# Half of the sums over x moved into attention, and gate steps from block 2 on

## The chip, the cores and the metric

The kernel runs on one core of a Trainium2 chip. The metric is the device time of one execution in microseconds; several executions of the kernel before are timed, and their median stands for it. One more execution is recorded by the profiler, and all rows quoted below come from it.

The engines are called as the profile calls them: PE (TensorE, matmuls), PEld (its weight loads), DVE (VectorE), ACT (ScalarE), POOL (GpSimd) and SP (SyncE, which here only issues DMAs). Every engine works through its own list of instructions in order; an instruction that must wait holds up all that stand behind it in that list. POOL both computes and issues DMAs, so a DMA on POOL that waits holds up POOL's arithmetic too.

## The reference, cut to what matters

All arrays are float32; x is 512 positions by 1024 features, one batch, one layer.

```python
h = rms_norm(x, norm_mix_g)
cb, cc, cin, q, k, v, f_logit, g_logit = split(h @ w_in)
u = causal_dwconv(cc * cin, conv_mix_w)              # 3 taps
y_conv = (cb * u) @ w_out_conv                       # 512 -> 1024
o = softmax(q.k / sqrt(64) + F[t] - F[s]) @ v        # s <= t, 8 heads of 64, F = cumsum(log_sigmoid(f))
y_attn = o @ w_out_attn                              # 512 -> 1024
g_conv, g_attn = split(sigmoid(g_logit + b_gate))    # 2 x 1024
x = x + (g_conv * y_conv + g_attn * y_attn) @ w_o
a, b = split(causal_dwconv(rms_norm(x) @ w_up, conv_ffn_w))   # 2 x 2816
x = x + (silu(a) * b) @ w_down
return rms_norm(x)
```

What matters here are the two gate projections: 1024 features in, two times 1024 out. They are computed in eight blocks j of 128 output features; a block needs one 128-wide piece of `g_conv` and one of `g_attn`.

## The kernel before

Features lie on the 128 partitions, positions along the free axis, so x is held as eight slabs of 128 x 512. Every matmul is made precise by splitting both sides into a high and a low part and adding three products (high weight by high x, low weight by high x, high weight by low x; `mm3`, L278, and `passes`, L296). One matmul is a 128x128 weight tile on 256 columns. Of x, scaled by the norm's gains, the high part `xgh` and the low part `xgl` are made once at the start. Weights are streamed by SP in an order fixed by the list `stream`; each chunk lands in one of five buffers `raw`, ACT copies it to `wh` (L245) and DVE subtracts to get `wl` (L249). `wh` and `wl` have two buffers each, so a chunk can be split while the one before it is multiplied. `proj` multiplies one chunk of 128 output features: 48 matmuls.

The stages in order:

1. **Start.** SP asks for `vec` (a table of per-feature constants, with the first half of the first slab of x in it), v weights and x slabs (L409 to L417): first in turn, and from slab 4 on all the rest of x ahead of the rest of the v weights. The v projection runs over the eight slabs.
2. **Attention.** q and k of heads 0 to 3, then 32 units of scores, softmax, transposes and products with v (`scores`, `transp`, `attend`). Between the units `fill` puts the halves of other projections: the conv branch (its products z and y on POOL, L569 and L579; its taps `u` on ACT and DVE, L548), the remaining q and k, and last the two gates of block 0. Three banks of PSUM (0, 1, 2) go round for these projections; before that, q1's result is in bank 0 and k1's in bank 1, and DVE reads q1's with L525 (`t_q`).
3. **Eight mix blocks.** Block j has its two gates, then `yc` (conv branch out) and `ya` (attention out) from the chunk `mix{j}`, then sigmoid, products and their sum (`ml`, `mh`).
4. **Output projection, FFN up, FFN down, final norm**, which this change doesn't touch.

The gates come in two ways. The plain way, blocks 1 and 2 (`GS = 3` is the first block not done so; block 0's gates belong to attention), is two `proj`: 96 matmuls. The other way, blocks 3 to 7 (`gate_pair`), is a 2-by-2 block product with seven products in place of eight (Winograd's form): 84 matmuls. It needs sums over weight blocks and sums over x blocks.

The weight sums are made in DRAM, with no engine: for a group of two steps, SP issues a copy (L132), POOL an accumulating DMA (L135), SP a copy, POOL an accumulating DMA, SP a copy, POOL an accumulating DMA, each one waiting for the one before. One of these six operations is issued at each `tick()`; there is a tick in each of the 32 attention units and then one at some of the weight chunks. The operations of two groups alternate (`zip` over two groups). A gate step then loads its chunk `P` (weights as they are, 384 KB) and its chunk `F` (sums, 512 KB).

The x sums: for each pair q of x slabs (four pairs) `x_load` (L777) asks POOL for the two slabs again from DRAM, `x_forms` scales them on ACT (L782), makes four sums t1 to t4 on DVE (L786 to L789) in a tile `tq`, and splits them into `txh` (ACT, L790) and `txl` (DVE, L791). All of it lies after attention: `x_load(0)` and `x_load(1)` at block 0, `x_forms` of pairs 0 to 3 behind the four plain projections of blocks 1 and 2, one each. The slabs' buffers are of the tag `mt` and can only be used when attention's own tiles have been given back.

The order on each engine is set when the program is built: most instructions keep the order in which the code names them, `after_split()` ties what is named inside it to stand behind the newest weight split, and the rest is ordered by the scheduler.

## Time and profile before

| | |
|---|---|
| runs of the kernel before | 704.12, 705.13, 705.40 us; median 705.13 |
| the profiled execution | 707.72 us, of which the span of the records is 706.0 |
| PE busy | 694.1 us, 98% |
| DVE busy | 494.1 us, 70% |
| ACT busy | 340.2 us, 48% |
| POOL busy | 155.8 us, 22% |
| PE by the chain that ended last | 92% of the span |
| attention with its projections, by the order of PE's rows | to 189.78 us |
| block 1: two plain gates | 189.78 to 204.77 us, 15.0 |
| block 2: two plain gates | 210.21 to 221.09 us, 10.9 |
| block 3: first gate step | 226.53 to 236.05 us, 9.5 |

Times inside the span are counted from its start. Granted clock (PEclk) is the TensorE clock that the throttle granted, 1.00 being full speed. A row of the timeline gives start, duration, engine, line, operation, output and inputs, and in brackets how long the engine was idle before and what ended that; a row of the chain gives start, duration, engine, line and output.

### The profile page before, as it was taken

How to read it: one execution, taken by the hardware profiler on the slowest of the kernel's cores; microseconds unless marked ns; L12 is line 12 of the kernel's file. 1: busy time of each engine (PE TensorE's matmuls, PEld its weight loads, DVE VectorE, ACT ScalarE, POOL GpSimd, SP SyncE). 2: the span in 40 equal slices, each digit the busy share in tenths (PEclk: the TensorE clock that was granted, in tenths of full speed). 3: DMA queues.
4: the chain of work that ended last, by engine and by line, in shares of the span. 5: the costliest groups of instructions: out<-in, count | busy, mean ns of one | idle time of the engine just before them, and what ended most of it. 6: DMA issues, size and time to landing. Idle time of an engine off the chain costs nothing.

```text
span 706.0 us, 14566 instructions
## 1 busy us (share of the span) xinstructions
PE 694.1 (98%) x6017; PEld 692.2 (98%) x6017; DVE 494.1 (70%) x790; ACT 340.2 (48%) x538; POOL 155.8 (22%) x177
## 2 busy tenths in 40 slices
PE   9999999999989999999999999999999999999995
PEld 9999999999989999999999999999999999999995
DVE  6677777765586777764368777777774677877853
ACT  6664655544474444444354444545443344544642
POOL 4125645435221010224412122120000111100002
PEclk9999999999999999999999999999999999999998
DMA  8534776847864696866566675537765233224503
GB/s 280 167 130 99 178 205 149 197 86 214 208 179 128 180 243 212 278 208 186 103 156 166 193 144 167 143 83 231 206 201 155 90 100 111 84 83 130 177 1 120
DMA packets 49682, 112.42 MB, mean 159 GB/s; under 512 B 4656, under 2 KB 21168, under 8 KB 49616
## 3 DMA queue, kind: packets, MB, share of 16 engines
q1 hardware_dynamic: 35776, 91.89, 40.4%
q0 software_dynamic: 12576, 18.39, 16.2%
q10 hardware_dynamic: 1264, 1.22, 0.5%
q8 instruction: 47, 0.77, 0.5%
q14 instruction: 19, 0.16, 0.1%
HBM read 109.31 MB, written 30.41 MB: 198 GB/s over the span
## 4 chain that ended last, share of the span: by engine, by line
PE 92%; DMA 3%; DVE 1%; ACT 1%; issue 1%; POOL 1%; DVEq 0%; POOLq 0%; ACTq 0%
PE p_up L278 26%; PE dn L296 11%; PE p_in L278 10%; PE p_up L296 8%; PE gs L296 7%; PE p_wo L278 6%; PE yc L296 3%; PE ya L278 3%; PE p_g L278 3%; PE pd L278 2%; PE pa L457 2%; DMA sum<-in_wst_dram 2%; PE pb L459 2%; PE p_q L278 2%; PE p_k L278 2%; PE o L638 1%
## 5 line engine op out<-in xcount | busy, mean ns | idle before, releaser
L278 PE MATMUL p_up<-x1h,wh_up 128*128 128x256 f32 x536 | 104.6, 276 | 0.0
L278 PE MATMUL p_up<-x1h,wl_up 128*128 128x256 f32 x536 | 104.4, 276 | 0.0
L278 PE MATMUL p_up<-x1l,wh_up 128*128 128x256 f32 x536 | 104.3, 276 | 0.0
L245 ACT ACTIVATE wh_up<-raw_up 128x1024 fp32r<-128x1024 f32 x44 | 46.7, 1060 | 89.1 <-PE p_up L278 68.8
L278 PEld LDWEIGHTS p_up<-x1h,wh_up 128*128 128x128 f32 x536 | 80.8, 188 | 0.0
L278 PEld LDWEIGHTS p_up<-x1h,wl_up 128*128 128x128 f32 x536 | 80.7, 188 | 0.0
L278 PEld LDWEIGHTS p_up<-x1l,wh_up 128*128 128x128 f32 x536 | 80.7, 188 | 0.0
L135 POOL DMA_DIRECT2D sum<-in_wst_dram x42 | 44.9, 1080 | 108.6 <-DMA sum<-sum 79.2
L249 DVE TENSOR_TENSOR wl_up<-raw_up,wh_up 128x1024 fp32r<-128x1024 f32 x44 | 53.8, 1223 | 20.6 <-ACT wh_up L245 20.6
L278 PE MATMUL p_in<-xgh,wh_in 128*128 128x256 f32 x288 | 56.9, 279 | 1.0 <-ACT wh_in L245 1.0
L278 PE MATMUL p_in<-xgh,wl_in 128*128 128x256 f32 x288 | 56.5, 277 | 0.0
L278 PE MATMUL p_in<-xgl,wh_in 128*128 128x256 f32 x288 | 56.5, 277 | 0.0
L245 ACT ACTIVATE wh_F<-raw_F 128x1024 fp32r<-128x1024 f32 x27 | 28.7, 1064 | 51.3 <-PE ya L278 22.9
L963 DVE TENSOR_TENSOR fz<-p_up,rb_n 128x512 f32<-128x512 f32 x44 | 30.2, 689 | 31.6 <-PE p_up L278 31.6
L976 POOL TENSOR_TENSOR ge<-fu,fu 128x512 f32<-128x512 f32 x11 | 17.1, 1551 | 150.4 <-DVE fu L552 137.5
L278 PEld LDWEIGHTS p_in<-xgh,wh_in 128*128 128x128 f32 x288 | 44.7, 188 | 1.9 <-ACT wh_in L245 1.2
L249 DVE TENSOR_TENSOR wl_F<-raw_F,wh_F 128x1024 fp32r<-128x1024 f32 x27 | 33.0, 1224 | 16.6 <-ACT wh_F L245 16.6
L278 PEld LDWEIGHTS p_in<-xgl,wh_in 128*128 128x128 f32 x288 | 43.6, 188 | 0.0
L278 PEld LDWEIGHTS p_in<-xgh,wl_in 128*128 128x128 f32 x288 | 43.5, 188 | 0.0
L296 PE MATMUL p_up<-x1h,wh_up 128*128 128x256 f32 x168 | 40.3, 277 | 0.0
L296 PE MATMUL p_up<-x1l,wh_up 128*128 128x256 f32 x168 | 40.2, 276 | 0.0
L249 DVE TENSOR_TENSOR wl_in<-raw_in,wh_in 128x1024 fp32r<-128x1024 f32 x26 | 32.2, 1239 | 5.9 <-ACT wh_in L245 5.5
(307 smaller groups left out, 2045.6 us busy)
## 6 DMA issues: line engine op xcount, KB each, us to landing
raw_up<-in_wup_dram SPq DMA_DIRECT2D x44, 512.0 KB, 3.5
raw_F<-sum SPq DMA_DIRECT2D x27, 512.0 KB, 4.7
raw_in<-in_win_dram SPq DMA_DIRECT2D x26, 512.0 KB, 4.2
raw_P<-in_wst_dram SPq DMA_DIRECT2D x27, 384.0 KB, 4.6
sum<-in_wst_dram POOLq DMA_DIRECT2D x27, 256.0 KB, 5.1
sum<-in_wst_dram SPq DMA_DIRECT2D x13, 512.0 KB, 5.9
sum<-in_wst_dram POOLq DMA_DIRECT2D x13, 512.0 KB, 7.3
sum<-sum SPq DMA_DIRECT2D x26, 256.0 KB, 3.8
```

What stands on the lines that cost most here:

```text
L135: return lambda: keep(nc.gpsimd.dma_start(dst, src, accum_op=ALU.add))
L245: ins = nc.scalar.activation(hi, raw, AF.Copy)
L249: ins = nc.vector.tensor_sub(lo, raw, hi.bitcast(F32))
L278: keep(nc.tensor.matmul(out[:, cs], w, x[:, cs], start=start and i == 0 and c == 0, stop=stop and i == 2 and c == len(cut) - 1,))
L296: keep(nc.tensor.matmul(out, wl if x == 1 else wh, xl if x == 2 else xh, start=opens and bk not in seen, stop=closes and bk not in left,))
L457: keep(nc.tensor.matmul(pa[t][:, :VW], xt, w[:, :VW], start=start, stop=stop))
L459: keep(nc.tensor.matmul(pb[t], xt, w[:, VW:], start=start and t % 2 == 0, stop=stop and t % 2 == 1))
L638: keep(nc.tensor.matmul(o[:, os_], vv[:, kb, pr, e, :], x[:, kb, cs], start=e == 0 and kb == 0 and i == 0, stop=e == 1 and kb == nk - 1 an ...
L963: nc.vector.tensor_mul(z, p, rb2)
L976: keep(nc.gpsimd.tensor_mul(ge, a.rearrange(halves_of, h=2), b.rearrange(halves_of, h=2)))
```

## The change

- `GS` goes from 3 to 2: block 2's two plain projections become a gate step. Its weight sums are one more group, so 36 in place of 30 operations on gate sums are spread over the ticks, and now three groups alternate in place of two.
- The x sums of pairs 0 and 1 move into attention. The slab pairs have tiles of their own, `xq` (two buffers, in a pool that exists from the start); x loads are asked for at units 2 and 6, scaling and sums (`x_sums`) at units 18 and 26, in place, and the splits `txh`, `txl` (`x_parts`) at block 0. In POOL's list the two loads stand among the memsets of the start. Pairs 2 and 3 are asked for at block 0, behind those splits, and their sums and splits come behind block 1's two plain projections.
- Room for this: `tq` goes, `mt` has 5 buffers in place of 6, `os` and `sq` one in place of two, `zn` uses one of the `pp` buffers.
- At the start x slabs and v weights are asked for in turn to the end (`AHEAD` 4, still five `raw` buffers), the first transfer holds half of slab 0 and the gains (264 columns, in a `pp` buffer), and the whole of `vec` (187 columns) comes after x.
- The ring of PSUM banks for attention's projections starts at bank 2: (2, 0, 1) in place of (0, 1, 2).

**ACT at the end of attention and in block 0 and 1.** `oth` is attention's last result, `g0`, `g8`, `g1`, `g9` are gates (8 and up: of the attention branch), `wh_in29` is the second plain chunk of block 1. Before:

```order
L649 ACTIVATE oth_106<-os31_2573 128x256
L782 ACTIVATE xq00_2592<-xq00_2592,vec_64 128x512
L803 ACT_TABLE_LOAD
L803 ACTIVATE g0_2600<-g0_2600,vec_64 128x512
L803 ACTIVATE g8_2603<-g8_2603,vec_64 128x512
L245 ACTIVATE wh_in29_2713<-raw_in29_2385 128x1024
L782 ACTIVATE xq01_2593<-xq01_2593,vec_64 128x512
L782 ACTIVATE xq10_2596<-xq10_2596,vec_64 128x512
L869 ACTIVATE mh_2590<-g0_2600 128x512
L782 ACTIVATE xq11_2597<-xq11_2597,vec_64 128x512
L245 ACTIVATE wh_mix1_2720<-raw_mix1_2477 128x1024
L790 ACTIVATE txh_2584<-tq0_2729 128x1024
L803 ACTIVATE g1_2724<-g1_2724,vec_64 128x512
```

Now:

```order
L670 ACTIVATE oth_107<-os31_2591 128x256
L801 ACTIVATE txh_2602<-xq0_889 128x1024
L815 ACT_TABLE_LOAD
L815 ACTIVATE g0_2610<-g0_2610,vec_64 128x512
L815 ACTIVATE g8_2613<-g8_2613,vec_64 128x512
L801 ACTIVATE txh_2602<-xq1_1070 128x1024
L244 ACTIVATE wh_in29_2731<-raw_in29_2313 128x1024
L882 ACTIVATE mh_2608<-g0_2610 128x512
L244 ACTIVATE wh_mix1_2738<-raw_mix1_2405 128x1024
L382 ACTIVATE xq2_2618<-xq2_2618,vec_64 128x512 x2
L815 ACTIVATE g1_2742<-g1_2742,vec_64 128x512
L801 ACTIVATE txh_2602<-xq2_2618 128x1024
```

Four scalings of single slabs (L782) stood around the table load, the sigmoids and `wh_in29`; now the two splits of pairs 0 and 1 stand there, and the scalings of pair 2 stand behind `wh_mix1`.

**POOL at the end of attention.** `sum` are the weight-sum groups, `z3` and `y3` the last products of the conv branch, `pp` the softmax normalisations. Before:

```order
L135 DMA sum4_88<-in_wst_dram 256x1x256
L607 TENSOR_SCALAR pp302_2199<-pp302_2199,m302_2197 128x384
L607 TENSOR_SCALAR pp312_2264<-pp312_2264,m312_2262 128x384
L135 DMA sum4_88<-in_wst_dram 256x1x256
L569 TENSOR_TENSOR z3_2299<-z3_2299,cc3_2186 128x512
L607 TENSOR_SCALAR pp303_2316<-pp303_2316,m303_2314 128x512
L607 TENSOR_SCALAR pp313_2356<-pp313_2356,m313_2354 128x512
L579 TENSOR_TENSOR y3_2391<-y3_2391,u3_2300 128x512
L135 DMA sum5_89<-in_wst_dram 256x1x512
L135 DMA sum6_90<-in_wst_dram 256x1x512
L777 DMA xq00_2592<-in_xT_dram 128x512
L777 DMA xq01_2593<-in_xT_dram 128x512
```

Now:

```order
L134 DMA sum3_87<-in_wst_dram 256x1x256
L628 TENSOR_SCALAR pp302_2219<-pp302_2219,m302_2217 128x384
L134 DMA sum4_88<-in_wst_dram 256x1x256
L628 TENSOR_SCALAR pp312_2284<-pp312_2284,m312_2282 128x384
L134 DMA sum5_89<-in_wst_dram 256x1x256
L590 TENSOR_TENSOR z3_2319<-z3_2319,cc3_2206 128x512
L628 TENSOR_SCALAR pp303_2336<-pp303_2336,m303_2334 128x512
L628 TENSOR_SCALAR pp313_2376<-pp313_2376,m313_2374 128x512
L600 TENSOR_TENSOR y3_2411<-y3_2411,u3_2320 128x512
L134 DMA sum3_87<-in_wst_dram 256x1x256
L376 DMA xq2_2618<-in_xT_dram 128x1024
L376 DMA xq3_2622<-in_xT_dram 128x1024
```

Between two operations of one group there are now two of other groups rather than one or none, and the x loads that are left (pairs 2 and 3, one DMA for each pair) stand behind the third operation of group 3.

**DVE in block 1, behind its first gate.** `wl_P17` and `wl_F17` belong to the first half of block 2's new gate step, `g9` is block 1's second gate. Before:

```order
L249 TENSOR_TENSOR wl_in22_2793<-raw_in22_2479,wh_in22_2792 128x1024
L802 TENSOR_TENSOR g9_2796<-p_g11_2740,rb_n1_539 128x512
L791 TENSOR_TENSOR txl_2585<-tq1_2801,txh_2584 128x1024
L866 TENSOR_TENSOR g1_2724<-g1_2724,yc1_2812 128x512
L787 TENSOR_TENSOR tq2_2935<-xq21_2737,xq20_2736 128x256
L788 SCALAR_TENSOR_TENSOR tq2_2935<-tq2_2935,xq21_2737 128x256
L789 SCALAR_TENSOR_TENSOR tq2_2935<-tq2_2935,xq21_2737 128x256
L867 TENSOR_TENSOR g9_2796<-g9_2796,ya1_2813 128x512
L786 TENSOR_TENSOR tq3_3002<-xq30_2808 128x256
L868 TENSOR_TENSOR g1_2724<-g1_2724,g9_2796 128x512
L249 TENSOR_TENSOR wl_in30_2920<-raw_in30_2549,wh_in30_2919 128x1024
```

Now:

```order
L248 TENSOR_TENSOR wl_P17_2805<-raw_P17_2497,wh_P17_2804 128x768
L814 TENSOR_TENSOR g9_2808<-p_g11_2753,rb_n1_543 128x512
L384 TENSOR_TENSOR xq3_2622<-xq3_2622 128x256
L879 TENSOR_TENSOR g1_2742<-g1_2742,yc1_2819 128x512
L385 TENSOR_TENSOR xq3_2622<-xq3_2622 128x256
L386 SCALAR_TENSOR_TENSOR xq3_2622<-xq3_2622 128x256
L387 SCALAR_TENSOR_TENSOR xq3_2622<-xq3_2622 128x256
L880 TENSOR_TENSOR g9_2808<-g9_2808,ya1_2820 128x512
L802 TENSOR_TENSOR txl_2603<-xq3_2622,txh_2602 128x1024
L881 TENSOR_TENSOR g1_2742<-g1_2742,g9_2808 128x512
L248 TENSOR_TENSOR wl_F17_2900<-raw_F17_2567,wh_F17_2899 128x1024
```

The split of block 2's plain chunk `in30` (and of `in22`) is replaced by those of `P17` and `F17`, with pair 3's sums and split ahead of `wl_F17`.

In the rows headed "now" the line numbers are those of the changed kernel, up to 21 higher or 1 lower than in the kernel before. The diff, cut to its core:

```diff
--- before.py
+++ after.py
@@ -22,9 +22,9 @@
-AHEAD = 3
+AHEAD = 4
 LOOK = 7
-NRAW = 5
+NRAW = AHEAD + 1
...
@@ -50,7 +49,7 @@
-GS = 3
+GS = 2
@@ -144,8 +143,8 @@
         ]
 
     for i0, i1 in ((0, ngate), (ngate, len(groups))):
-        for i in range(i0, i1, 2):
-            todo += [op for ops in zip(*(group(x) for x in range(i, min(i + 2, i1)))) for op in ops]
+        for i in range(i0, i1, 3):
+            todo += [op for ops in zip(*(group(x) for x in range(i, min(i + 3, i1)))) for op in ops]
 
     def tick():
         if todo:
@@ -370,6 +369,23 @@
     ych = abp.tile([P, 4, S], F32R, tag="ych", name="ych")
     ycl = abp.tile([P, 4, S], F32R, tag="ycl", name="ycl")
 
+    xqs = {}
+
+    def x_load(q):
+        xqs[q] = abp.tile([P, 2, S], F32, tag="xq", name=f"xq{q}", bufs=2)
+        nc.gpsimd.dma_start(xqs[q], xT[:, 2 * q : 2 * q + 2, :])
+
+    def x_sums(q):
+
+        x = xqs[q]
+        for i in range(2):
+            nc.scalar.activation(x[:, i, :], x[:, i, :], AF.Copy, scale=col(G1 + 2 * q + i))
+        (t1, t3), (t4, t2) = (b11, b12), (b21, b22) = [[x[:, i, h] for h in halves] for i in range(2)]
+        nc.vector.tensor_sub(t1, b11, b12)
+        nc.vector.tensor_sub(t3, b22, b12)
+        nc.vector.scalar_tensor_tensor(t2, t1, -1.0, b22, op0=ALU.mult, op1=ALU.subtract)
+        nc.vector.scalar_tensor_tensor(t4, t2, -1.0, b21, op0=ALU.mult, op1=ALU.subtract)
+
     at = ExitStack()
     ap = at.enter_context(tc.tile_pool(name="ap", bufs=1, side="right"))
 
@@ -406,18 +422,19 @@
         keep(nc.sync.dma_start(xs[kb][:, cs], xT[:, kb, cs]))
 
 
-    keep(nc.sync.dma_start(vec[:, :CM], vecs[:, :CM]))
+    x0 = ap.tile([P, S], F32, tag="pp", name="x0", bufs=NPP)[:, : S // 2 + KB]
+    keep(nc.sync.dma_start(x0, vecs[:, NV:]))
     load(0)
     load_x(0, halves[1])
     for kb in range(1, AHEAD + 1):
         load_x(kb)
         load(kb)
-    for kb in range(AHEAD + 1, KB):
-        load_x(kb)
-    keep(nc.sync.dma_start(vec[:, CM:], vecs[:, CM:]))
 
     def x_of(kb, cs):
-        return vec[:, XV : XV + S // 2] if kb == 0 and cs.start == 0 and cs.stop == S // 2 else xs[kb][:, cs]
+        return x0[:, : S // 2] if kb == 0 and cs.start == 0 and cs.stop == S // 2 else xs[kb][:, cs]
+
+    def g1(kb):
+        return x0[:, S // 2 + kb : S // 2 + kb + 1]
 
     def square_x(kb):
         if kb == 0:
@@ -435,17 +452,21 @@
 
         def x_hi():
             for cs in cuts:
-                keep(nc.scalar.activation(xgh[:, kb, cs], x_of(kb, cs), AF.Copy, scale=col(G1 + kb)))
+                keep(nc.scalar.activation(xgh[:, kb, cs], x_of(kb, cs), AF.Copy, scale=g1(kb)))
 
 
         if kb == 1:
             x_hi()
         wh, wl = chunk(f"v{kb}")
+        if AHEAD + kb < KB - 1:
+            load_x(AHEAD + kb + 1)
+        elif AHEAD + kb == KB - 1:
+            keep(nc.sync.dma_start(vec, vecs[:, :NV]))
         if kb != 1:
             x_hi()
         for cs in cuts:
             keep(nc.vector.scalar_tensor_tensor(
-                xgl[:, kb, cs], x_of(kb, cs), col(G1 + kb), xgh.bitcast(F32)[:, kb, cs],
+                xgl[:, kb, cs], x_of(kb, cs), g1(kb), xgh.bitcast(F32)[:, kb, cs],
                 op0=ALU.mult, op1=ALU.subtract,
             ))
         for i in squares[kb]:
...
@@ -660,7 +681,8 @@
 
 
     fr = ap.tile([4 * H, S], F32R, tag="fr", name="fr")
-    zn = ap.tile([P, NT, 4, H], F32, tag="zn", name="zn")
+    zn = ap.tile([P, S], F32, tag="pp", name="zn", bufs=NPP)[:, : NT * 4 * H]
+    zn = zn.rearrange("p (t a b) -> p t a b", t=NT, a=4)
     for t in range(NT):
         src = pa[t][:, 4 * HD : VW].unsqueeze(1).to_broadcast([P, 4, H])
         nc.vector.tensor_scalar_mul(zn[:, t], src, rc1[:, t : t + 1])
@@ -725,7 +747,7 @@
         evac_qk(0, False)(st[1])
     run_all(proj(13, "q1", evac_qk(1, True), ring(0)))
     run_all(proj(17, "k1", evac_qk(1, False), ring(1)))
-    acc, bank_s, bank_t = ring(0, 1, 2), ring(3, 4), ring(5, 6)
+    acc, bank_s, bank_t = ring(2, 0, 1), ring(3, 4), ring(5, 6)
 
     fill = []
     gp = []
@@ -743,6 +765,8 @@
         if i < n:
             scores(*units[i])
             tick()
+        if i in (2, 6):
+            x_load(i // 6)
         take = 1 if i < n + LA - 1 else len(fill)
         for _ in range(min(take, len(fill))):
             fill.pop(0)()
@@ -752,6 +776,9 @@
             pr, e, qb = units[i - LA]
             if e == 1 and qb % 2 == 1:
                 attend(pr, qb // 2)
+        if i in (18, 26):
+            with after_split():
+                x_sums(i // 26)
     at.close()
 
 
@@ -767,26 +794,10 @@
     ml = mp.tile([P, KB, S], F32R, tag="ml", name="ml")
 
     def mt(name):
-        return mp.tile([P, S], F32, tag="mt", name=name, bufs=6)
-
-    xqs = {}
-
-    def x_load(q):
-        xqs[q] = [mt(f"xq{q}{i}") for i in range(2)]
-        for i, x in enumerate(xqs[q]):
-            nc.gpsimd.dma_start(x, xT[:, 2 * q + i, :])
-
-    def x_forms(q):
-        x = xqs.pop(q)
-        for i in range(2):
-            nc.scalar.activation(x[i], x[i], AF.Copy, scale=col(G1 + 2 * q + i))
-        (b11, b12), (b21, b22) = [[x[i][:, h] for h in halves] for i in range(2)]
-        t = gxp.tile([P, 4, 2 * P], F32, tag="tq", name=f"tq{q}", bufs=2)
-        t1, t2, t3, t4 = (t[:, i, :] for i in range(4))
-        nc.vector.tensor_sub(t1, b11, b12)
-        nc.vector.tensor_sub(t3, b22, b12)
-        nc.vector.scalar_tensor_tensor(t2, t1, -1.0, b22, op0=ALU.mult, op1=ALU.subtract)
-        nc.vector.scalar_tensor_tensor(t4, t2, -1.0, b21, op0=ALU.mult, op1=ALU.subtract)
+        return mp.tile([P, S], F32, tag="mt", name=name, bufs=5)
+
+    def x_parts(q):
+        t = xqs.pop(q).rearrange("p a (h c) -> p (a h) c", h=2)
         nc.scalar.activation(txh[:, q], t, AF.Copy)
         nc.vector.tensor_sub(txl[:, q], t, txh.bitcast(F32)[:, q])
 
@@ -794,7 +805,8 @@
         if g < 3:
             m, h = ((0, 0), (1, 0), (1, 1))[g]
             return xgh[:, 2 * q + m, halves[h]], xgl[:, 2 * q + m, halves[h]]
-        return txh[:, q, g - 3, :], txl[:, q, g - 3, :]
+        i = (0, 3, 1, 2)[g - 3]
+        return txh[:, q, i, :], txl[:, q, i, :]
 
     def evac_gate(idx, dst):
         def f(p):
@@ -837,17 +849,18 @@
     for j in range(KB):
         gs = []
         if j == 0:
-            x_load(0)
-            x_load(1)
             evac_gate(0, gs)(gp[0])
             evac_gate(8, gs)(gp[1])
+            with after_split():
+                for q in range(2):
+                    x_parts(q)
+                    x_load(q + 2)
         elif j < GS:
             for c, ev in enumerate((evac_gate(j, gs), evac_gate(8 + j, gs))):
                 run_all(proj(20 + 8 * c + j, f"g{c}{j}", ev, acc))
-                q = 2 * j - 2 + c
-                x_forms(q)
-                if q < 2:
-                    x_load(q + 2)
+                with after_split():
+                    x_sums(2 + c)
+                    x_parts(2 + c)
         else:
             gs += gate_pair(j)
         wh, wl = chunk(f"mix{j}")
...
```

16 lines of the change are left out of this document (8 added, 8 removed).

## Prediction, made before the changed kernel ran

> **What bounds the kernel now.** I read the page first (its slices), then what PE waits for, then the chain of what ended last around the changed blocks, then the timeline there.
>
> ```profile
> PEclk9999999999999999999999999999999999999998
> ```
>
> The profiled execution took 707.72 us, 1.72 more than its span, and 2.59 more than the median of the runs. PE is busy for 98% of the span by the table above, and the granted clock is full at this resolution, so time goes only where PE has fewer matmuls, waits less, or runs faster than it did in a short stretch that the 40 slices hide. PE's two longest waits, with sum, times, longest:
>
> ```profile
> PE p_g L278 <- DVE wl_in L249: 1.1, 1, 1.1
> PE p_in L278 <- ACT wh_in L245: 1.0, 1, 1.0
> ```
>
> Each is one event, so it can be found. The chain through blocks 1 to 3 (start, duration):
>
> ```profile
> 192.37 1.28 ACT L803
> 193.66 1.35 ACT g L803 x2
> ...
> 197.64 7.13 PE p_g L278 x46
> 204.77 2.72 PE yc L296 x24
> ...
> 210.21 10.88 PE p_g L278 x96
> ...
> 226.53 9.52 PE gs L296 x84
> ```
>
> Block 2's gates run with no gap: 96 matmuls in 10.88 us, 0.1133 each; a gate step's 84 run at the same pace. Block 1's have gaps, behind ACT's table load and sigmoids. Its timeline:
>
> ```profile
> 186.11 0.42 ACT L649 ACTIVATE oth<-os 128x256 fp32r<-128x256 f32 x1 [0.49 <-DVE os L648]
> 187.68 2.23 POOL L777 DMA_DIRECT2D xq<-in_xT_dram  x4 [9.85 <-PE yc L296]
> 191.63 0.72 ACT L782 ACTIVATE xq<-xq,vec 128x512 f32<-128x512 f32 x1 [5.10 <-DMA xq<-in_xT_dram]
> 194.91 1.04 ACT L245 ACTIVATE wh_in<-raw_in 128x1024 fp32r<-128x1024 f32 x1
> 189.78 0.39 PE L278 MATMUL p_g<-xgh,wh_in 128*128 128x256 f32 x2
> 196.00 0.50 PE L278 MATMUL p_g<-xgh,wh_in 128*128 128x256 f32 x2 [0.62 <-ACT wh_in L245]
> 197.64 0.50 PE L278 MATMUL p_g<-xgh,wl_in 128*128 128x256 f32 x2 [1.14 <-DVE wl_in L249]
> ```
>
> POOL can ask for x only when attention has given its tiles back. ACT's first scaling waits 5.10 us for that load, with the table load, two sigmoids and `wh_in29` queued behind it. `wh_in29` comes at 195.95, though the first chunk was multiplied by 189.78 + 5.44 = 195.22; `wl_in29` follows on DVE. Behind the gap the clock falls (columns: stretch, length, then busy PE, PEld, DVE, ACT, POOL, clock, DMA share, GB/s):
>
> ```profile
> 195.10:198.33 3.23, 1.47 (x10) 1.07 (x9) 3.20 (x6) 3.23 (x6) 0.12 (x1) 1.00 0.00 0
> 198.33:201.60 3.27, 3.27 (x18) 3.27 (x17) 3.27 (x7) 2.29 (x3) 2.07 (x3) 0.51 0.92 280
> ```
>
> With PE busy for 1.47 of 3.23 us, the next 3.27 us were granted 0.51, a loss of 0.49 x 3.27 = 1.60.
>
> **The change, part by part.**
>
> *Fewer matmuls.* Block 2 has 84 for 96: 10.88 - 9.52 = **1.36** us. That is certain as long as the step is fed.
>
> *Block 1's stall.* From 189.78 to 204.77 are 14.99 us for work of 10.88: 4.11 lost, 1.60 by the clock and 2.51 by the two waits with their edges. Now ACT has two splits `txh` there, of sums made in attention, and no load to wait for. From the end of `oth` at 186.53 the list is `txh` 1.06 (by the row of L790 below), table load 1.28, two sigmoids 1.35, `txh` 1.06 and `wh_in29` 1.04: 5.79, so 192.3. DVE's `wl_in29` is the later one: behind `ya0`, which PE ends at 189.78, stand a product and a sum, `txl`, `ml` and `wl_in29`, by the rows below 0.65 + 0.65 + 1.22 + 0.65 + 1.23 = 4.4, about 194.2 and at worst 195.05 if `ml` waits for `mh` behind `wh_in29`. It is needed at 195.22 + 0.23 = 195.45. So 0.4 is to spare, and past that each us of delay is a us of PE. I take all **4.11**; the lower end is 2.51, if the slow clock has another cause and stays.
>
> *The ring of banks.* The first projection of attention, `p_in4`, starts late:
>
> ```profile
> 54.16 2.98 PE p_in L278 x24
> ...
> 52.19 1.23 DVE L249 TENSOR_TENSOR wl_in<-raw_in,wh_in 128x1024 fp32r<-128x1024 f32 x1 [0.41 <-ACT wh_in L245]
> 53.02 1.06 ACT L245 ACTIVATE wh_in<-raw_in 128x1024 fp32r<-128x1024 f32 x1 [0.87 <-PE p_k L278]
> 53.33 0.68 DVE L525 SCALAR_TENSOR_TENSOR t_q<-p_q,rb_n 128x512 f32<-128x512 f32 x1
> ```
>
> PE had ended k1 by 53.02 (that releases ACT). The ACT row named as releaser, ending at 54.08, is the split of the next chunk, which `p_in4` doesn't read; what it needs is bank 0, and `t_q` reads q1 from there until 54.01. With bank 2 first, PE starts at 53.02, does two matmuls and waits for `wl_in4` until 53.42, about 0.3. So 1.14 becomes 0.3: **0.8**, with ends 0 (the ACT row is the true cause) and 1.14.
>
> *Weight sums in threes.* Near the end of attention PE waits once more:
>
> ```profile
> 167.49 1.05 POOL L135 DMA_DIRECT2D sum<-in_wst_dram  x1 [6.36 <-DMA sum<-sum]
> 169.90 0.72 ACT L548 ACTIVATE u<-z,vec 128x512 f32<-128x512 f32 x1 [6.24 <-POOL z L569]
> 170.86 0.39 PE L278 MATMUL p_in<-xgl,wh_in 128*128 128x256 f32 x2
> 171.89 0.52 PE L623 MATMUL tp<-ident,pp 128*128 128x128 f32 x3 [0.64 <-DVE ptl L627]
> ```
>
> POOL stood 6.36 us at an accumulating DMA whose sum wasn't copied yet; `z3` came behind it, ACT waited for `z3` 6.24 us at `u`, and the split that frees the transposes' bank (`ptl`, the releaser of PE's 0.64) stood behind `u`. From 170.86 two matmuls take 0.23, so PE lost 171.89 - 171.09 = 0.80. The landings (KB each, us from issue):
>
> ```profile
> sum<-in_wst_dram POOLq DMA_DIRECT2D x27, 256.0 KB, 5.1
> ...
> sum<-sum SPq DMA_DIRECT2D x26, 256.0 KB, 3.8
> ```
>
> Attention's 37 rounds last from 54.16 to 184.34 (block 1's start less the 5.44 of `yc` and `ya`), 3.5 us each. Of five gate groups taken by twos, group 4 alternates with none: its operations follow each other in 3.5 us, less than a copy's 3.8 or an addition's 5.1. Six groups in threes put them 10.5 us apart, so POOL should reach `z3` without a wait. Gain **0.8**, lower end 0.
>
> *Block 2's new feeding.* Its step starts at 189.78 + 10.88 + 5.44 = 206.10. Durations by the nearest rows:
>
> ```profile
> 187.02 1.29 DVE L802 TENSOR_TENSOR g<-p_in,rb_n 128x512 f32<-128x512 f32 x2
> 197.50 0.42 DVE L787 TENSOR_TENSOR tq<-xq,xq 128x256 f32<-128x256 f32 x1
> 199.56 1.06 ACT L790 ACTIVATE txh<-tq 128x1024 fp32r<-128x1024 f32 x1 [0.31 <-DVE tq L789]
> 201.18 1.22 DVE L791 TENSOR_TENSOR txl<-tq,txh 128x1024 fp32r<-128x1024 f32 x1
> ```
>
> On DVE: `wl_mix1` to 197.6, gate 0.65, four sums 1.68, `txl` 1.22 (to 202.3 with the waits for ACT), `wl_P17` (768 columns, at most a `wl_in`'s 1.23), `g9` at 203.5, pair 3's sums. Then `g9` times `ya1` needs `ya1`, which PE ends at 206.10; behind it stand 0.65, `txl` 1.22, 0.65 and `wl_F17` 1.23: 206.10 + 3.75 = 209.85. `P17` has 18 matmuls, and of `F17`'s 24 the 16 with its high part come first, so `wl_F17` is needed at 206.10 + 34 x 0.1133 = 209.95. That is level, so I charge **0.3**; the ends are 0 and 1.5 (one more instruction ahead, or `ya1` a little late). Pair 3's parts are first needed with `P18`, at 206.10 + 42 x 0.1133 = 210.86, and `txl` gives them at 208.0.
>
> *The x loads.* Of pairs 2 and 3, the loads are now issued when the splits of pairs 0 and 1 have read their buffers, about 189.8 and 193.6. The nearest row for the landing (KB each, us to landing):
>
> ```profile
> xq<-in_xT_dram POOLq DMA_DIRECT2D x8, 256.0 KB, 4.6
> ```
>
> A load is twice as large now, so 4.6 to 9.2: pair 2 by 194.4 to 199.0 (ACT wants it about 196.4), pair 3 by 198.2 to 202.8 (wanted 201.7, and harmless until about 205.5). Cover is the plain gates of block 1; without it every us counts.
>
> The Trainium skill, "SBUF — State Buffer", section "Who interferes with whom" and the one on the bandwidth intuition, speaks against asking on POOL under a busy DVE: POOL's descriptors wait while DVE holds the port they share, about 620 ns alone against 3100. By that figure, an estimate from the page, the two loads would land about 2.5 us later and cost up to 1 us more; no run so far shows such a wait here, the rows above put 2.23 us to four issues.
>
> *Work put into attention.* Each of units 18 and 26 gets four sums, 1.68 us, on DVE and two scalings, 1.44, on ACT.
>
> ```profile
> 113.00:130.00 17.00, 17.00 (x148) 17.00 (x147) 13.47 (x30) 10.55 (x24) 8.65 (x12) 1.00 0.74 167
> ```
>
> DVE has 3.53 of 17 us free there, ACT 6.45, and PE doesn't wait. **0**; were the cover gone, the 1.68 of each would show.
>
> *The start.* Two 512 KB loads now go out among the first memsets, into the time in which x and the v weights come in:
>
> ```profile
> 10.00:20.00 10.00, 10.00 (x85) 10.00 (x84) 9.05 (x14) 7.26 (x13) 0.00 (x0) 1.00 0.88 299
> ```
>
> DMA is 0.88 busy and PE has no gap. 1.05 MB at about 0.4 MB per us delays what follows by 2.6 us at most; x and v weights arrive several us ahead of use from slab 4 on, and slab 3 with about 0.4. I take **0**; the upper end is 2.6. Loading x and v in turn brings the weights earlier and works the other way.
>
> Everything behind block 3 keeps its instructions. Sum: 1.36 + 4.11 + 0.8 + 0.8 - 0.3 = 6.77; 707.72 - 6.77 = 700.95 in the profiled execution, and 705.13 - 6.77 = **698.4** for the median. The ends of the terms give 1.36 + 2.51 - 1.5 = 2.4 (702.7) and 1.36 + 4.11 + 1.14 + 0.8 = 7.4 (697.7).
>
> The Trainium skill, "TensorE: Matmul & The Clock Gate", section "Why this matters for your kernels", gives the clock up only after idle gaps of about 3.4 us. The longest gap here is 1.14 us, yet the clock fell to 0.51; by the page 1.60 of block 1's loss would not be the stall's and the sum would be 5.2.
>
> **The rivals.**
>
> *Small stalls stay.* If ACT's `wh_in`, which the wait's row names, and `ptl` ahead of 171.89 are limits of their own, 1.6 is not gained: 700.0. Against it, the instructions don't read `wh_in8`.
>
> *The slow clock stays.* If the 0.51 of 198.33 to 201.60 doesn't come from the gaps ahead of it, it comes again, here or elsewhere, for 1.60: 700.0. Against it, the page's clock slices show no other slow stretch in these blocks. That is what the Trainium skill's page on the clock gate, named above, would make of it.
>
> *Pairs 2 and 3 land late.* With each load 2.5 us later, `txl` of pair 3 would come at 209 to 211 and push `wl_F17` by about 1: 699.4. For it, only a doubled size; against it, the 4.6 of the row above.
>
> *Block 2 starves.* Were `wl_F17` 1.3 us late with `wl_P18` behind it, PE would idle as at 195 to 198 and the clock could follow: 1.3 + 1.1 (half the slow stretch) to 2.5 + 1.6, 2.4 to 4.1, so 700.5 to 702.2. For it speaks that DVE has no spare there; against it, that the wait is one subtraction.
>
> *The start collides.* Up to 2.6: 701.0. Against it, weights come earlier by the new order.
>
> *Slower.* POOL's list is in order: the loads of pairs 2 and 3 stand behind the third addition of group 3, which waits for SP's copy as at 167.49. If they land after 212.3, which is 205.5 plus the gain of 6.8, each us past that is a us lost, and block 2's step waits for pair 3. The 6.36 us wait is for it; but the additions stand there about 10 us apart, and the copy is asked for before 180. A landing at 214 would give 706.8.
>
> **How the numbers follow.** Forecast 0.54, 698.4, its own range 697.4 to 699.6; small stalls stay 0.15 (700.0); slow clock stays 0.06 (700.0); pairs 2 and 3 late 0.03 (699.4); block 2 starves 0.12 (701.3); start collides 0.06 (701.0); slower 0.04, of which a quarter ends within no change, as do the worst of starving and colliding together. A measurement here tells 0.2%, 1.4 us, from no change, and the runs before differ by 1.28. The range goes from 696.6, one such spread below the best sum, to 702.2, the dear end of starving. Faster 0.94, same 0.03, slower 0.03.
>
> **What would show it.** Right: block 1's gates in one row of about 10.9 us at clock 1.00 with no 5.10 us wait on ACT; `p_in4` starting within 0.4 us of k1's end; POOL's additions in attention without multi-us waits ahead of `z3`; 84 matmuls in block 2 in 9.5 to 9.9. Wrong: PE idle before `F17` or `P18`, a clock below 1.00 in block 2, or gaps before 30 us.

## The result, and the profile after

| | before | changed |
|---|---|---|
| median | 705.19 us (704.12 to 705.40, 4 runs) | 701.18 us (700.69 to 701.32, 4 runs) |
| ratio | | 0.9937, 95% interval 0.9922 to 0.9952 |
| profiled execution | 707.72 us, span 706.0 | 700.69 us, span 698.9 |

The changed kernel is 4.0 us faster, 0.6%. The forecast was 6.8 us less than the median: 698.4, with a range of 696.6 to 702.2. The two profiled executions are 7.0 us apart, though, and the forecast for the profiled one was 700.95 against 700.69. So the working nearly fits the pair of traces, in part by luck (below), and most of the 2.8 us by which the median is off is how far the execution that was profiled before stood from the others. Two disturbed executions, one of the run with the scalings behind `wh_in29` (997.58 us, the profiled one) and one of the kernel before (1958.47 us), are left out of all medians and comparisons of durations here.

What PE waited for in the profile after (sum, times, longest):

```profile
PE warm L103 <- DVE ones L95: 1.0, 1, 1.0
PE pa L478 <- ACT wh_v L244: 0.6, 1, 0.6
PE pc_n L336 <- ACT sq L1187: 0.3, 1, 0.3
PE pb_n L350 <- POOL rc_n L343: 0.2, 1, 0.2
```

The two waits in block 1, the one ahead of `p_in` and the one for `ptl` are gone; a wait of 0.6 for the second v weight, at 7 us, is new. Block 1's gates, `yc` and `ya` of block 1, and block 2's gate step (columns as in the prediction):

```profile
187.73:198.61 10.88, 10.88 (x98) 10.88 (x97) 8.30 (x12) 6.82 (x10) 3.31 (x4) 1.00 0.67 159
198.61:204.05 5.44, 5.44 (x50) 5.44 (x49) 4.71 (x8) 3.31 (x5) 0.00 (x0) 1.00 0.90 240
204.05:214.24 10.19, 10.14 (x86) 9.84 (x85) 7.58 (x9) 6.21 (x7) 1.02 (x1) 1.00 0.69 145
```

Block 1 takes its 10.88 with no gap at full clock. Block 2's step takes 10.19 where 84 matmuls at pace need 9.52: 0.67 is lost, all of it between the end of `P17` and the low part of `F17`. The rows there, PE's, ACT's and DVE's:

```profile
205.98 0.28 PE L295 MATMUL gs<-txh,wl_P 128*128 128x256 f32 x1
206.31 0.39 PE L295 MATMUL gs<-xgh,wh_F 128*128 128x256 f32 x1
```

```profile
204.24 1.06 ACT L801 ACTIVATE txh<-xq 128x1024 fp32r<-128x1024 f32 x1 [1.52 <-DVE xq L387]
205.21 1.04 ACT L244 ACTIVATE wh_F<-raw_F 128x1024 fp32r<-128x1024 f32 x1
205.34 1.22 DVE L802 TENSOR_TENSOR txl<-xq,txh 128x1024 fp32r<-128x1024 f32 x1 [0.33 <-ACT txh L801]
207.08 1.22 DVE L248 TENSOR_TENSOR wl_F<-raw_F,wh_F 128x1024 fp32r<-128x1024 f32 x1
```

`wh_F17` stands on ACT behind pair 3's `txh`, which waited 1.52 us for pair 3's sums; at `F17`'s first matmuls PE lost 0.33 us. On DVE `wl_F17` stands behind pair 3's `txl` and ended at 208.30; its first matmul started at 208.35, and PE lost another 0.18 there. The rest is a slightly slower pace in between. In attention, the first projection and the last product `z`:

```profile
52.66 0.40 PE L277 MATMUL p_in<-xgh,wh_in 128*128 128x256 f32 x2
53.13 0.50 PE L277 MATMUL p_in<-xgh,wl_in 128*128 128x256 f32 x2
```

```profile
163.35 1.29 POOL L590 TENSOR_TENSOR z<-z,cc 128x512 f32<-128x512 f32 x1 [2.71 <-DVE z L589]
```

`p_in` starts right behind the scores, two matmuls and then a gap of 0.24 for `wl_in`. `z` waits for its own input from DVE and not for a DMA.

### The profile page after: what moved, and what is told of

It reads as the page before. It is cut to its first block, busy times and chain, and to the rows that moved or that the text cites. A ratio compares the mean times of both kernels' runs of the same rounds, so it can differ in the third digit from the quotient of the medians.

```text
span 698.9 us, 14573 instructions
## 1 busy us (share of the span) xinstructions
PE 690.2 (99%) x6005; PEld 688.1 (98%) x6005; DVE 498.3 (71%) x797; ACT 341.8 (49%) x541; POOL 156.4 (22%) x176
## 4 chain that ended last, share of the span: by engine, by line
PE 92%; DVE 2%; ACT 2%; issue 1%; DMA 1%; ACTq 0%; SPq 0%; POOL 0%; DVEq 0%
PE p_up L277 26%; PE p_in L277 14%; PE dn L295 12%; PE p_up L295 8%; PE gs L295 8%; PE p_wo L277 6%; PE yc L295 3%; PE ya L277 3%; PE pd L277 2%; PE o L659 2%; PE pa L478 2%; PE pb L480 1%; PE tp L644 1%; PE pdB L277 1%; PE pdA L277 1%
## 5 line engine op out<-in xcount | busy, mean ns | idle before, releaser
L134 POOL DMA_DIRECT2D sum<-in_wst_dram x45 | 47.1, 1122 | 116.4 <-DMA sum<-sum 88.8
L244 ACT ACTIVATE wh_F<-raw_F 128x1024 fp32r<-128x1024 f32 x29 | 30.8, 1063 | 54.6 <-PE ya L277 25.9
L248 DVE TENSOR_TENSOR wl_F<-raw_F,wh_F 128x1024 fp32r<-128x1024 f32 x29 | 35.5, 1223 | 17.5 <-ACT wh_F L244 17.5
L244 ACT ACTIVATE wh_P<-raw_P 128x768 fp32r<-128x768 f32 x29 | 24.4, 842 | 26.1 <-PE dn L295 14.1
```

The costliest lines, as they stand in the source:

```text
L134: return lambda: keep(nc.gpsimd.dma_start(dst, src, accum_op=ALU.add))
L244: ins = nc.scalar.activation(hi, raw, AF.Copy)
L248: ins = nc.vector.tensor_sub(lo, raw, hi.bitcast(F32))
```

## The experiments

Each was timed against runs of the kernel before on the same chip; the medians of those runs were 705.26 us (for the first two runs below, block 2 plain and pair 3's split behind `F17`), 705.14 (the old start, the scalings behind `wh_in29`, the copy on ACT, the early loads held in the changed kernel) and 705.62 (the others). The changed kernel wasn't timed again with them, and where two edited kernels differ by 0.7 to 0.9 us their intervals overlap, so such differences rest on the rows as much as on the times.

**The kernel before, again.** No edit.

> The kernel before, unchanged, to see more executions of it with their spans and granted clocks. Theory: the profiled execution of 707.72 us was a dear one; in ordinary executions (705.1) block 1's plain gates take not 14.99 us but about 12.4, since the stretch at clock 0.51 (1.60 us) and part of the waits are missing, so the mean granted clock is 0.995 or 0.996 and not 0.993. Rival: block 1 takes 15 us in every execution, with the slow stretch and a mean clock of 0.993, and the 2.6 us lie at the start or the end of the span.

Measured: 705.39 us, ratio 0.9998 (0.9989 to 1.0007); this profile is of an execution of 704.65. Its waits, its rows in block 1 and its windows there:

```profile
PE p_g L278 <- DVE wl_in L249: 1.1, 1, 1.1
PE warm L104 <- DVE ones L96: 1.1, 1, 1.1
PE p_in L278 <- ACT wh_in L245: 1.0, 1, 1.0
PE tp L623 <- DVE ptl L627: 0.7, 1, 0.7
```

```profile
187.03 2.23 POOL L777 DMA_DIRECT2D xq<-in_xT_dram  x4 [9.83 <-PE yc L296]
190.20 0.72 ACT L782 ACTIVATE xq<-xq,vec 128x512 f32<-128x512 f32 x1 [4.32 <-DMA xq<-in_xT_dram]
193.48 1.05 ACT L245 ACTIVATE wh_in<-raw_in 128x1024 fp32r<-128x1024 f32 x1
```

```profile
189.13:201.58 12.45, 11.32 (x99) 11.07 (x98) 8.98 (x15) 9.99 (x13) 2.32 (x4) 1.00 0.55 173
194.80:198.10 3.30, 2.17 (x18) 1.97 (x18) 3.30 (x8) 3.03 (x5) 1.24 (x3) 1.00 0.24 39
198.10:201.40 3.30, 3.30 (x32) 3.30 (x31) 3.30 (x5) 2.20 (x3) 0.95 (x1) 1.00 1.02 332
```

Here the x load is in ACT's hands 3.17 us after its issue (187.03 to 190.20), not 3.95 (187.68 to 191.63). `wh_in29` is then just in time, the wait for it (0.79 with its edges) is missing, only the one for `wl_in29` is left, and the clock stays at 1.00. Block 1 takes 12.45 us and loses 1.57. In the prediction's trace it took 14.83 by the same rows (189.78 to 204.61) and lost 3.95; the 4.11 took the block's end from the chain. Of 60 executions of the kernel before 2 had a mean clock of 0.994 or less, as the 0.993 of the 707.72 us execution; they took 706.76 and 706.92. Three others took 706.94 to 707.47 at 0.996, so not every dear execution has the slow stretch. As far as one more profile and the clocks can show it, the theory holds: the trace that the prediction was made from was of a rare kind in the one place that its largest term came from.

**The early sums alone.** Of the change, only `x_load`, `x_sums` and `x_parts` for pairs 0 and 1 are kept (with the buffers, the new first transfer and `vec` behind x). The edit to the changed kernel, cut:

```diff
-GS = 2
+GS = 3
-        for i in range(i0, i1, 3):
+        for i in range(i0, i1, 2):
-    acc, ... = ring(2, 0, 1), ...
+    acc, ... = ring(0, 1, 2), ...
 # x slabs 4 to 7 again ahead of the v weights
```

> Of the change only the move of the x sums of pairs 0 and 1 into attention is kept; block 2's gates are plain as before, groups alternate by twos, the ring starts at bank 0, x is asked for at the start as before. If block 1 costs 15 us in ordinary executions too, this gains 4.1 us on the kernel before: 701.0. If ordinary executions lose only about 1.5 there, 703.6. In its profile block 1's gates take 10.9 us either way, and the idle 0.8 us at about 171 and the 1.1 us at about 53 are still there.

Measured: 704.59 us, ratio 0.9988 (0.9979 to 0.9997): 0.7 us gained, less than either theory. Its profile shows block 1 without a gap, and two waits that the kernel before hasn't got:

```profile
PE pa L477 <- ACT xgh L458: 0.8, 1, 0.8
PE pa L477 <- ACT wh_v L244: 0.6, 1, 0.6
```

The first is at 17 us (0.96 with its edge), in the v projection, and the first q matmul comes at 30.66 us, against 28.89 and 29.54 in the two profiles of the kernel before. The early x loads, issued at 8.09 and 9.33 us, are the suspects.

**The same with the early x loads later.** On the kernel above:

```diff
     def x_load(q):
         xqs[q] = ...
-        nc.gpsimd.dma_start(xqs[q], xT[:, 2 * q : 2 * q + 2, :])
+        keep(nc.gpsimd.dma_start(xqs[q], xT[:, 2 * q : 2 * q + 2, :]))
```

`keep` holds them to their place in the code, units 2 and 6; they are now issued at 64.55 and 78.35 us.

> The early sums alone, as in the run that kept nothing else of the change, but with the two early x loads held to units 2 and 6 of attention. If the start's wait at 17 us (0.96) was the early loads' doing, it is gone, and the time is 705.2 less block 1's ordinary 1.6, 703.6. If it is the order of x and v loads alone, the wait stays and the time is 704.5.

Measured: 703.11 us, ratio 0.9965 (0.9953 to 0.9977), clear of the 0.9988 (from 0.9979) of the run without the hold. Its waits in the v projection are one only:

```profile
PE p_in L277 <- ACT wh_in L244: 1.0, 1, 1.0
PE pa L477 <- ACT wh_v L244: 0.6, 1, 0.6
```

The wait at 17 us is gone, and the first q matmul is at 29.56 us. The other one, at 7 us, stays; it comes before the loads are issued and isn't theirs. So with the old order of x and v, two early loads of 512 KB cost about 1 us at the start, the rival called the start's collision. The 2.5 us below the kernel before are 0.9 more than block 1's 1.57. Its profile also lost only 0.20 at 171 us, against 0.80 and 0.83 in the two profiles of the kernel before; whether that is so in its other executions isn't known, nor what the rest is.

**The old start in the changed kernel.** x slabs 4 to 7, and the rest of `vec`, ahead of v weights 4 to 7 again, all else as changed (cut: the later requests for these slabs, one by one, go):

```diff
     for kb in range(1, AHEAD + 1):    # AHEAD = 3
         load_x(kb)
         load(kb)
+    for kb in range(AHEAD + 1, KB):
+        load_x(kb)
+    keep(nc.sync.dma_start(vec, vecs[:, :NV]))
```

> The changed kernel with x slabs 4 to 7 asked for ahead of v weights 4 to 7, and vec's rest ahead of them too, as in the kernel before; the early x loads stay among the first memsets. In the profile of the run with the early sums alone, which has this order, PE waited 0.96 us at 17 us for a slab or a weight. If the turn by turn order is what keeps the early x loads harmless, this is 0.7 to 1.0 slower than the changed kernel, 702.0, with that wait in its profile; otherwise 701.2.

Measured: 701.86 us, ratio 0.9955 (0.9942 to 0.9969), 0.7 above the changed kernel as expected, with the expected wait at 17 us (0.74 with its edge):

```profile
PE pa L477 <- ACT xgh L458: 0.6, 1, 0.6
```

The two intervals overlap, so it's the rows more than the time that show it: the first q matmul comes at 30.39 us, against 29.05 to 29.70 in the seven profiles with the new order, early loads among the memsets in five of them. Asking for x and v in turn is what pays for the early loads.

**Scalings behind `wh_in29`, loads no earlier.** On the kernel before:

```diff
         for i, x in enumerate(xqs[q]):
+            if q == 0 and i == 0:
+                nc.gpsimd.dma_start(x[:, :16], xT[:, 0, :16])
             nc.gpsimd.dma_start(x, xT[:, 2 * q + i, :])
```

> The kernel before, with one thing changed: the first of the four x loads behind attention is preceded by a small one of 16 columns into the same buffer, so that its data come later, and the order on ACT becomes table load, sigmoids, wh_in29 and only then the scalings of x. The loads come no earlier than before and no sum is moved into attention. If what costs block 1 is that ACT's list stands behind the x load, block 1's gates take 10.9 us and the time is 705.3 - 1.6 = 703.7. If it is the work of the x sums there, whatever its order, 705.3.

Measured: 703.51 us (702.78 to 704.37, 7 runs), ratio 0.9979 (0.9968 to 0.9990): 1.6 us gained by the medians and 1.5 by the ratio, as the first theory has it. Its profile shows the order on ACT that was meant, the table load, the sigmoids, `wh_in29` and then the scalings, but its durations can't be compared, so the size rests on the times. Block 1's stall is a matter of what stands ahead of `wh_in29` on ACT; its removal can be had without a single sum moved into attention. The last run below shows the same in its rows.

**One more copy on ACT in block 0.** On the kernel before:

```diff
             nc.vector.tensor_mul(g, p, rb1)
+            if idx == 0:
+                nc.scalar.activation(g, g, AF.Copy)
```

> The kernel before with one more copy of 128x512 on ACT (0.72 us) between the x load and wh_in29; it changes nothing in the result. Theory: the granted clock drops when PE is idle for more of some 3.3 us than about a third, which the 707.72 us execution reached (1.47 busy of 3.23) and ordinary ones don't (2.17 of 3.30). Then nearly every execution looks like that one: 0.7 to 0.8 of delay and 1.6 of slow clock, 707.6, with a clock of 0.51 behind the gap. Rival: the slow clock is chance and not the gap's, 706.0 with a clock of 1.00.

Measured: 705.60 us (704.99 to 707.73, 11 runs), ratio 1.0008 (0.9998 to 1.0019). The theory's 707.6 was wrong for the median: with 0.72 us of work ahead of `wh_in29` it is 0.5 higher, and the interval takes in both no change and the rival's 706.0. (The one profile lost only 0.18 at 171 us, so the copy's own price can't be read from the median.) But of the 11 executions 3 had a mean clock of 0.993 (706.35, 707.09, 707.73), against 2 of 60 of the kernel before. One of these was profiled:

```profile
194.60:197.90 3.30, 1.66 (x10) 1.26 (x9) 3.27 (x6) 3.30 (x5) 0.29 (x1) 0.93 0.00 0
197.90:201.20 3.30, 3.30 (x19) 3.30 (x18) 3.30 (x8) 1.93 (x4) 1.91 (x3) 0.56 0.99 308
```

```profile
PE p_g L278 <- DVE wl_in L249: 1.1, 1, 1.1
PE p_g L278 <- ACT wh_in L245: 0.5, 1, 0.5
```

The same two waits, the same slow stretch behind them. So with more delay the slow stretch is more frequent, 3 of 11 against 2 of 60, but not certain. Whether the share of PE's idle time alone decides it isn't shown, since no execution of this kernel with an ordinary clock was profiled. One execution of 707.71 had a clock of 0.998, so here too not every dear execution is one of these.

**Block 2 plain again.** On the changed kernel:

```diff
-GS = 2
+GS = 3
```

(and an `if j == 1:`, so that the sums of pairs 2 and 3 are still made once, behind block 1.)

> The changed kernel with block 2's two gates plain again (first gate step in block 3); all else stays. The step saves 1.36 us of matmuls and costs 0.67 of waits and edges in the profile of the changed kernel, so this should be 0.7 slower than it: 701.9. Were the waits in block 2 only in the profiled execution, 702.5; were the step worth nothing, 701.2.

Measured: 701.97 us, ratio 0.9953 (0.9940 to 0.9967): 0.8 above the changed kernel, as expected, though the intervals overlap. Its block 2 takes

```profile
204.33:215.21 10.88, 10.88 (x98) 10.88 (x97) 6.35 (x8) 4.43 (x5) 2.05 (x2) 1.00 0.75 177
```

so the step of 10.19 gains 0.69 of its 1.36. Behind PE's last row the profiles differ once more: from the last `pb_n` to the end of the span it is 7.50 to 7.63 us in six with a plain block 2, this one among them, and 7.14 to 7.28 in all seven with a gate step there. No run shows what makes these 0.3 us. This kernel has five groups, and in threes group 4 alternates with group 3; no wait stands at 171 us.

**Pair 3's split behind `F17`.** On the changed kernel:

```diff
                     x_sums(2 + c)
-                    x_parts(2 + c)
+                    if c == 0:
+                        x_parts(2)
+                    else:
+                        later.append((index of F17, 0.7, (), lambda: x_parts(3)))
```

> The changed kernel with pair 3's split into txh and txl put behind the split of F17 on ACT and DVE, so that wh_F17 doesn't stand behind a txh that waits for sums. If PE's 0.67 us in block 2 are the wait for wh_F17 and its edges, this is 0.3 to 0.7 faster than the changed kernel, 700.5 to 700.9, with no gap ahead of F17 in the profile. If the next wait takes its place (wl_F17, then txl of pair 3 for P18), 701.2.

Measured: 700.29 us, ratio 0.9930 (0.9918 to 0.9943), 0.9 below the changed kernel's median. The step:

```profile
204.44:213.96 9.52, 9.52 (x87) 9.52 (x86) 7.57 (x9) 6.11 (x7) 1.02 (x1) 1.00 0.72 173
```

0.67 of the 0.9 is this; no next wait took its place. Both losses in the rows above, at `wh_F17` and at `wl_F17`, are gone.

**The same with the early loads held to units 2 and 6**, by the `keep` shown above.

> The kernel with pair 3's split behind F17, and the two early x loads held to where the code asks for them, in units 2 and 6 of attention, rather than among the first memsets. If these loads hold up x slabs and v weights at the start, the v projection ends about as early as in the kernel before (first q matmul at 28.9 us rather than 29.5) and the time is 699.6. If the start's waits have other causes (at 7 us the loads are not yet issued), 700.3.

Measured: 699.87 us (699.72 to 700.34), ratio 0.9923 (0.9909 to 0.9938). It is the fastest kernel here, 1.3 below the changed one. Its first q matmul comes at 29.05 us, against 29.58 of the kernel without the hold, but the difference between the two profiles is the wait at 7 us (0.48 and 1.03 with edges), ahead of the loads' issue. The 0.4 us are within the two intervals, and that the hold brings them isn't shown.

**The ring from bank 0.** On the changed kernel:

```diff
-    acc, ... = ring(2, 0, 1), ...
+    acc, ... = ring(0, 1, 2), ...
```

> The changed kernel with the ring of attention's projection banks starting at bank 0 again. By the forecast's term the first projection waits for DVE's reading of q1 from bank 0: 0.8 us slower than the changed kernel, 702.0, with a gap of 1.1 to 1.2 us ahead of the first p_in in the profile. If the ACT row that the profile names is the cause, 701.2 and a gap of 0.3.

Measured: 701.95 us, ratio 0.9945 (0.9934 to 0.9957), 0.8 above the changed kernel as expected. The intervals overlap, but the gap of 1.16 is back:

```profile
53.03 0.28 PE L616 MATMUL s<-kb,qb 68*128 68x256 f32 x1
54.31 0.48 PE L277 MATMUL p_in<-xgh,wh_in 128*128 128x256 f32 x2 [0.99 <-ACT wh_in L244]
```

The row still names ACT's `wh_in`, which changed nothing with the ring; the bank did. The named releaser was only the last to end.

**Groups by twos.** On the changed kernel:

```diff
-        for i in range(i0, i1, 3):
+        for i in range(i0, i1, 2):
```

(and `min(i + 2, i1)` in the next line.)

> The changed kernel with the weight-sum groups alternating by twos again. It has six gate groups, so by twos none of them stands alone at the end of attention, and operations of a group are 7 us apart. If the wait at 171 us came from group 4 standing alone (3.5 us apart), no wait comes back and the time is 701.2. If threes are what is needed, POOL waits again and this is 0.8 slower, 702.0.

Measured: 700.97 us, ratio 0.9934 (0.9922 to 0.9946): no loss. POOL reaches `z` without a DMA ahead of it:

```profile
163.79 1.28 POOL L590 TENSOR_TENSOR z<-z,cc 128x512 f32<-128x512 f32 x1 [3.71 <-DVE z L589]
```

So it isn't the three that count: the sixth group, which block 2's step brings, gave group 4 a partner. Five profiles in which group 4 stands alone (five groups by twos) have POOL waiting 6.0 to 6.6 us at the addition ahead of `z`. The next run shows that a partner isn't enough.

**No early sums, block 2 still a gate step.** On the changed kernel:

```diff
         if j == 0:
+            for q in range(2):
+                x_load(q)
...
                 with after_split():
-                    x_sums(2 + c)
-                    x_parts(2 + c)
+                    x_sums(c); x_parts(c); x_load(c + 2)
+                    if c:
+                        for q in (2, 3):
+                            x_sums(q); x_parts(q)
```

(cut: the loads and sums in units 2, 6, 18 and 26, and the splits at block 0, go.)

> The changed kernel with no x sum in attention: pairs 0 and 1 are loaded at block 0 and summed behind block 1's two plain gates, pairs 2 and 3 are loaded when these are split and summed behind them; block 2 is a gate step. Block 1 has no stall here, since the scalings stand behind wh_in29. Pair 3 is then asked for at about 204 us, lands at 208.5, and has its parts at about 213, where P18 wants them at 208.8: 4 us of PE, and 1.6 more if the clock falls, so 705 to 707. If it is within 1 us of the changed kernel, the early sums weren't what block 2's step needs.

Measured: 715.76 us (713.86 to 716.92), ratio 1.0135 (1.0118 to 1.0153): the sign as expected, the size about three times that.

```profile
PE gs L295 <- ACT txh L796: 4.8, 2, 3.3
PE tp L644 <- DVE ptl L648: 2.6, 1, 2.6
PE gs L295 <- DVE txl L797: 1.8, 2, 0.9
```

```profile
212.00:216.00 4.00, 4.00 (x24) 4.00 (x23) 4.00 (x6) 2.49 (x5) 0.82 (x1) 0.57 0.79 178
223.00:227.40 4.40, 4.40 (x28) 4.40 (x28) 1.23 (x1) 1.28 (x2) 1.05 (x1) 0.66 0.59 197
```

```profile
168.28 1.03 POOL L134 DMA_DIRECT2D sum<-in_wst_dram  x1 [7.68 <-DMA sum<-sum]
168.86 1.76 POOL L590 TENSOR_TENSOR z<-z,cc 128x512 f32<-128x512 f32 x1
```

```profile
207.92 0.72 ACT L382 ACTIVATE xq<-xq,vec 128x512 f32<-128x512 f32 x1 [2.46 <-DMA xq<-in_xT_dram]
208.55 1.04 ACT L796 ACTIVATE txh<-xq 128x1024 fp32r<-128x1024 f32 x1
```

Pair 3 was late, and so was pair 1, which the expectation left out: its `txh` (208.55) stood on ACT behind a scaling of pair 2 that waited for its load. So PE waited in both halves of block 2's step and the clock fell behind each. And in this order the scheduler put an addition ahead of `z` again, though its group had partners, with a wait of 7.68 us and 2.6 us of PE; so not all of the 14.6 us are block 2's. With the sums this late, block 2's step isn't fed; whether another late order would feed it isn't shown. Block 1 doesn't need the early sums: here, with `wh_in29` ahead of the scalings, its gates took 10.88 us (190.48 to 201.36) at a clock of 1.00.

## Why the prediction was right and where it wasn't

The sign and the full range held, and so did the terms of the ring, the weight sums, the work put into attention and the start. Block 2's net gain came out at two thirds, and the largest term and the step from the trace to the median failed. The median lies outside the forecast's own range of 697.4 to 699.6, close to two rivals, block 2 starving (701.3) and the start colliding (701.0). Neither happened, so that the time fell there is chance. Of the signs named, the step's 10.19 us, PE's loss ahead of `F17` and a gap before 30 us spoke against it, all others for it.

- **Fewer matmuls, less the new feeding.** Forecast 1.36 - 0.3. The step lost 0.67, inside the ends of 0 and 1.5, and so 0.69 was left; the run with block 2 plain is 0.8 dearer. The prediction put the tight place at `wl_F17` on DVE, behind pair 3's `txl`. PE lost 0.18 there, and 0.33 earlier at `wh_F17` on ACT, behind pair 3's `txh`, which the prediction didn't follow; moving pair 3's split took both away. What it cost was right in kind: the wait for one split, no starving, and no fall of the clock.
- **Block 1.** "I take all 4.11" is the step that failed. Each part of the mechanism was as told: ACT's list behind the x load, then `wh_in29`, then `wl_in29`, then the clock. After the change none is left, and `wl_in29` ended at 193.00, 0.4 us ahead of its need at 193.40, as the prediction's worst case had it. But in an ordinary execution this costs 1.57 in the trace, and 1.6 by the times of the run that moved only the scalings. The lower end given, 2.51, left only the clock out. It should have gone down to the wait for `wl_in29` alone, since the other wait was a load that came 0.8 us later than in the second profile. The sign was in view: the profiled execution stood 2.59 above a median whose runs spread over 1.28, and one rare event of about that size (0.79 and 1.60) stood in its trace. The forecast subtracted it from the median, where it isn't.
- **The ring.** 0.8 forecast, 0.8 measured by undoing it, and the gap is back in the rows; the bank and not the named row was the cause.
- **Weight sums.** 0.8 forecast, and the loss of 0.80 at 171 us is gone from the profile. The reason given, group 4 alone, fits: five profiles with it have POOL's wait, and with a partner the wait is gone in seven of eight, by twos as well as by threes. It isn't the whole of it, since the eighth, without early sums, waited 7.68 us; the place that the scheduler gives the additions counts too. By how much it shortens an ordinary execution isn't settled: the two profiles of the kernel before lost 0.80 and 0.83 there, the other three with group 4 alone 0.62, 0.20 and 0.18.
- **The x loads of pairs 2 and 3** landed in time. The row for them in the profile after (KB each, us to landing):

```profile
xq<-in_xT_dram POOLq DMA_DIRECT2D x2, 512.0 KB, 4.2
```

  That is a little below the 4.6 to 9.2 given, with DVE busy for 8.30 of 10.88 us, and ACT's scalings at 194.34 and 199.87 waited for no load. The loads came no 2.5 us later, as the estimate by the Trainium skill would have had it. The figure behind it ("SBUF — State Buffer", section "A bandwidth-pool intuition that's wrong (but worth ruling out)") is for a load beside DVE's `tensor_copy`; in DVE's rows around the two issues (187.69 and 191.57) all are tensor_tensor, which the section "Who interferes with whom" tells apart as not stalling DMA. So the prediction stretched the page's figure to a case that it doesn't cover. The slower case, which hung on these loads, didn't come up.
- **The start.** Taken as 0, and no more is seen. In the changed kernel the first q matmul is at 29.20 us, and at 29.05 to 29.70 in all seven profiles with the new start, though a wait of 0.6 at 7 us is new. The old start had it at 28.89 and 29.54 in the two profiles of the kernel before, and at 29.61 in the run with one more copy. The collision is real (0.7 to 1.0) with the old order of the loads and hidden by the new one, as the prediction guessed without a price.

The second profile of the kernel before has a span of 702.9 us, the changed kernel's 698.9. By PE's rows the 4.0 us between them are 1.57 in block 1, 1.71 in attention (the ring and the weight sums), 0.69 in block 2 and 0.36 behind PE's last row, which no run explains, less 0.31 at the start, which is within what executions differ by. Between the two profiled executions, 7.1 us of span, block 1 gives 3.95, and the start and the end add 0.75 that the forecast didn't have, while block 2 gave 0.4 less than forecast. So 700.95 came closer to 700.69 than its terms did.

Two slips in the working bear on nothing: half of the slow stretch costs 0.8 us and not 1.1, and 697.7 less 1.28 is 696.4 and not 696.6.

## What to carry to other kernels

Before a stall that is seen once in one execution goes into a sum, ask whether that execution is an ordinary one: when it stands apart from the median by more than the runs spread, look for the rare event in its trace and take the term without it as one end. A wait whose named releaser isn't an input of the waiting instruction points to something else that ended a little earlier, such as a buffer or a bank. A DMA that is only "asked for early" can be hoisted to the very start, where it competes with the loads on which the first matmuls hang; order those, or hold the early one back.

## What the runs showed of the hardware

A load of 256 KB that came 0.8 us later went with about 2.4 us more in block 1 (14.83 against 12.45): PE waited once more, and behind the waits the clock fell. Each time it stayed at half for 3.4 us: by windows of 0.2 us or less from 198.4 to 201.8 in the prediction's trace, from 197.4 to 200.8 with the copy on ACT, from 212.3 to 215.8 and from 222.6 to 226.0 without early sums. So the prediction's 3.27 us, and the 1.60 lost in them, are a little short; 3.4 us at half clock lose 1.7.

In the first two of these kernels the stretch came behind gaps of which none was longer than 1.42 us from one matmul's start to the next: with PE busy for 1.47 of 3.23 us or 1.66 of 3.30 the next 3.3 us were at 0.51 and 0.56, while with 2.17 of 3.30 they were at 1.00. The Trainium skill, "TensorE: Matmul & The Clock Gate", section "What's actually happening", has the clock fall after an idle window of about 3.4 us, one that runs free of the program. The length of the slow stretches, 3.4 us, agrees with such a window, and that one kernel had a low mean clock in 3 of 11 executions would fit one that runs free; that the window must be wholly idle doesn't agree with the 1.47 and 1.66 us of work here. What share of work is enough, and where the windows' edges lay, no run here shows.
